# Low halves of one token group's weights: from GpSimd's subtract to VectorE's

## The chip, the cores and the metric

The kernel runs on one core of one Trainium2 chip. A core has five instruction queues: TensorE (PE, matrix products into PSUM), VectorE (DVE), ScalarE (ACT), GpSimd (POOL) and SyncE (SP, which here only issues DMAs). Each queue executes its own instructions in order and they meet through semaphores. The metric is the device time of one execution in microseconds (us); lower is better.

## The reference, cut to what matters

A two-layer decoder step for 1024 prompt tokens and 64 sample tokens, model width 1024, everything in float32. Layer 0 is a gated short convolution beside a 4-head attention over 256 memory rows; layer 1 is latent attention with a paged cache (8192 past positions for each of 8 sequences) beside the same kind of memory attention.

```python
def conv_layer(x, hist, mem_k, mem_v, mem_q_g, norm_g, w_in, conv_w, w_out):
    proj = rms_norm(x, norm_g) @ w_in
    u, gb, gc, q_mem, z = jnp.split(proj, CONV_SPLITS, axis=-1)
    full = jnp.concatenate([hist.astype(x.dtype), gc * u], axis=1)
    conv = sum(conv_w[j] * full[:, j:j + t] for j in range(CONV_WIDTH))
    y_conv = gb * conv
    q = rms_norm(q_mem.reshape(b, t, MEM_HEADS, MEM_HEAD_DIM), mem_q_g)
    y_mem = mem_attend(q, mem_k, mem_v)
    out = jnp.concatenate([y_conv, y_mem], axis=-1) * jax.nn.silu(z)
    return x + out @ w_out, full[:, t:]
...
def mla_layer(x, pos, attend, mem_k, mem_v, ...):
    proj = rms_norm(x, norm_g) @ w_in        # then q, latent kv, memory q and gate z
    o_lat = attend(q_abs, q_pe, ckv, kpe, kscale)
    ...
    return x + out @ w_out, ckv, kpe, kscale
```

## The kernel before

Each large product is made of three matmuls on rounded operands. A float32 operand `a` is split into a high half `h` (ACT rounds `a` to the fp32r type, line 183 in `split`) and a low half `l = a - h` (`sub`, line 179, one subtract with two SBUF inputs). `mm3` (lines 189 to 191) then adds `wh*xh`, `wh*xl` and `wl*xh` in PSUM, so line 191 is the one matmul of the three that needs the weight's low half, line 190 the one that needs the activations' low half.

The prompt is cut in two token groups. Group A holds 256 prompt tokens and the 64 sample tokens (320 columns in a matmul), group B the other 768 prompt tokens (two chunks of 384). Both groups stream the same weights from HBM, each on its own: layer 0's input weights in 40 units of 128x1024 (tiles `wri` raw, `whi` high, `wli` low), layer 0's output weights in 16 units of 128x768 (`wro`, `who`, `wlo`), layer 1's input weights in 19 units of 128x1024 (`wri` again). `Stream.get(i)` (line 318) splits unit i+1 and loads unit i+2 while unit i is used. There are two buffers of each tile: ACT may overwrite `whi` only when PE has finished the unit that lay there, and SP may reload `wri` only when both halves of the unit that lay there have been made.

Which engine makes the halves is set by small tables: the first entry of `A_ENG` (group A), `W_ENG` (group B), `M_ENG` (memory weights, `wlm`) and `O_ENG` (the last output weights) names the engine of the low halves, `"v"` VectorE or `"g"` GpSimd; the second, `"a"`, says that ACT makes the high ones. Group A's low halves are made on GpSimd and group B's on VectorE. In the layer 0 norm, `norm_T2` (line 263) makes the low halves of the eight activation tiles `xL`, every second one by `le`, which is GpSimd. `split_y` (line 712) makes the low halves of twelve output tiles, block 6 (`YG`) on GpSimd.

The program is written as generators that run in two strands: the left one holds the memory keys and values (`mem_kv`), then group B, then the prompt's latent attention; the right one holds group A, then the samples' paged attention. `interleave` (line 1791) alternates the strands by nominal costs in the `yield`s, and when the program is built the framework's scheduler lays the recorded instructions of all strands into one fixed order for each engine, by its own cost model. A change of an instruction's engine therefore moves its neighbours too. On VectorE the order around the change holds, besides the subtracts, chains of very short instructions on [128, 2] tiles (the inverse square roots, lines 202 to 206, tiles `rsq`, `mrs`, `strxb`, `ksr`), the convolution (lines 659 to 682, tiles `vb`, `cv`, `yr`), the softmax steps (lines 493 to 500) and the square sums of group B's norm (line 259, `sqaxb`). GpSimd, besides the subtracts, makes short copies of the convolution's history (lines 648 to 668) and issues the gathers of the paged cache (line 1078).

Of the kernel before, what the change touches and what calls it, by code (L numbers as in the profile page):

```python
# [49 lines left out]
NATB = 4  # L50
RECB = 2
M_ENG = ("vvgv", "a")
A_ENG = ("g", "a")
SCL = "vaaaaaaa"
PSP = "ggg"
W_ENG = ("v", "a")
# [5 lines left out]
VI = (2, 3, 4, 5)  # L62
SLAG = 1
O_ENG = ("g", "a")
YG = (6,)
YORD = [(0, 2)] + [(b, x) for b in (11, 0, 1, 2, 3, 4, 5, 6, 7) for x in range(2)]
YLB = 6
O1I = (0, 1, 2, 4, 6)
# [17 lines left out]
VG0, VG1, VGM, VGQL, VGQ, VGK, VMQ, VCW = 0, 8, 16, 32, 35, 36, 37, 39  # L86
# [6 lines left out]
def build(nc, tc, I, O):  # L93
# [30 lines left out]
    NB = {"v": V, "g": G}[NBE]  # L124
# [26 lines left out]
    def vcol(i):  # L151
        return vec[:, i:i + 1]
# [28 lines left out]
    def split(h, l, src, he="a", le="v"):  # L181
        if he == "a":
            A.activation(h, src, AF.Copy)  # L183
        else:
            V.tensor_copy(h, src)
        sub(V if le == "v" else G, l, src, h)
# [57 lines left out]
        for k in range(8):  # L244
            split_g(xH[:, k, :], xL[:, k, :], xk(k), gcol + k)

    def norm_T(pt, x, gcol, tiles, Tn, xH, xL, tag, le="g", ae=None, load=None):

        acc = pt.tile([128, Tn], F, name="sqa" + tag, tag="sqa")
        A.activation(acc, x[:, 0, :], AF.Square)  # L250
        for k in range(1, 8):
            if load:
                load(k + XAH)
            sq = pt.tile([128, Tn], F, name="sq" + tag, tag="sq", bufs=2)
            if ae and SQB[k % 2] == "g":
                G.tensor_tensor(out=sq, in0=x[:, k, :], in1=x[:, k, :], op=ALU.mult)
            else:
                A.activation(sq, x[:, k, :], AF.Square)
            (ae or V).tensor_tensor(out=acc, in0=acc, in1=sq, op=ALU.add)
            yield 0.0015 * Tn  # L260
        yield from norm_T2(pt, lambda k: x[:, k, :], acc, gcol, tiles, Tn, xH, xL, tag, le)

    def norm_T2(pt, xk, acc, gcol, tiles, Tn, xH, xL, tag, le="g"):
        r = stat_r(pt, [acc], tiles, D, tag)[1]
        yield NY
        rb = bcast_tok(pt, r, tiles, Tn, tag)
        yield 3.0
        for k in range(8):
            xn = pt.tile([128, Tn], F, name="xn" + tag, tag="xn", bufs=2)
            x = xk(k)  # L270
            for c0, n, ps in rb:
                V.scalar_tensor_tensor(out=xn[:, c0:c0 + n], in0=x[:, c0:c0 + n], scalar=vcol(gcol + k), in1=ps[:, 0:n], op0=ALU.mult, op1=ALU.mult)
            split(xH[:, k, :], xL[:, k, :], xn, "a", le if k % 2 else "v")
            yield 0.002 * Tn

    class Stream:
# [351 lines left out]
    def in0(g, xH, xL, ytile, done, pq, last=None):  # L628
# [3 lines left out]
        order = list(range(40)) if g.sample else order  # L632
        ws = Stream(pw, pw, [I["wi0"][u] for u in order], 1024, "i0", *(A_ENG if g.sample else W_ENG))
        pp = P.new("p1c" + str(g.p0))
# [86 lines left out]
    def out0(g, get, xsrc, acc, keep, px=None, held=None, wpre=()):  # L721
# [7 lines left out]
        def weights():  # L729
            p = P.new("p2w" + str(g.p0))  # L730
            ws = Stream(p, p, [I["wo0"][u][:, 768 * j:768 * (j + 1)] for u in range(8) for j in ((1, 0) if px and u == 7 else (0, 1))], 768, "o0", *(A_ENG if g.sample else W_ENG), bufs=2)
            ws.raw.update(enumerate(wpre))
# [946 lines left out]
    def group_b(g, xin):  # L1679
# [3 lines left out]
        xH = px.tile([128, 8, g.T], R, name="xH")  # L1683
        xL = px.tile([128, 8, g.T], R, name="xL")
        pt = L.new("ptb")
        x = pt.tile([128, 8, g.T], F, name="x")
# [5 lines left out]
        for k in range(XAH + 1):  # L1692
            load(k)
            yield 0.5
        yield from norm_T(pt, x, VG0, g.tiles, g.T, xH, xL, "xb", "g", NB, load)
        L.close(1)
        py = L.new("pyb")

# [53 lines left out]
    def layer1(g, N, xH, xL, pq, start=None):  # L1752
# [3 lines left out]
        pw = N.new("pnw" + tag)  # L1756
        ws = Stream(pw, pw, [I["wi1"][u] for u in range(19)], 1024, "i1", *(A_ENG if g.sample else W_ENG))
        if start:
# [193 lines left out]
```

## Time and profile before

| | us |
|---|---|
| median of 3 runs (lowest to highest) | 2034.68 (2033.48 to 2039.29) |
| the profiled execution's own time | 2020.94 |
| span of its instructions | 2019.1 |
| PE busy / VectorE / ScalarE / GpSimd | 1919.3 / 990.9 / 744.9 / 665.0 |

The profiled execution is one execution on the chip, recorded instruction by instruction. Its time is 13.7 us below the median of the runs, so sums over the trace are made against its own time. "Span" runs from the first to the last instruction. PE is busy in 95% of it. [...]

### The profile page before, as it was taken

Reading aid. Unit: us, or ns where it says so; the run is one execution under the profiler, and the core shown is the slowest. Engines: PE = TensorE matmul, PEld = TensorE weight load, DVE = VectorE, ACT = ScalarE, POOL = GpSimd, SP = SyncE. Lnnn points to the kernel's source line nnn. Section 1 sums busy time; section 2 is a strip of 40 time slices with the busy share of each in tenths; the row PEclk is TensorE's granted clock in tenths of the full one; section 3 lists DMA queues with packets and bytes.
Section 4 is the critical chain, followed back from the end, with each engine's and each line's share of the span. In section 5 each row is a group of like instructions: output and inputs, shape, how many; then the busy total and the mean of one; then the engine's idle time right before and its main releaser. Section 6 shows DMA issues by size and latency. Waiting matters only on the chain. (4 is left out here: it accounts for less than half of the span.)

```text
span 2019.1 us, 35721 instructions
## 1 busy us (share of the span) xinstructions
PE 1919.3 (95%) x12508; PEld 1655.5 (82%) x12508; DVE 990.9 (49%) x2578; ACT 744.9 (37%) x1499; POOL 665.0 (33%) x588
## 2 busy tenths in 40 slices
PE   6987999998999999999999999999998899998999
PEld 6987998988997877777788776777787687787999
DVE  7559454456653534444323444445456556657300
ACT  6434323333321133333222422333343666667300
POOL 4544432422220213333333334332322333432220
PEclk8999999989999999999999999999999999999999
DMA  6553535552446378787998888887852211113532
GB/s 223 169 193 91 176 98 211 146 158 87 154 142 217 101 242 284 226 293 250 313 322 286 268 278 293 265 258 247 283 169 69 84 57 58 65 43 129 183 95 73
DMA packets 192884, 368.28 MB, mean 182 GB/s; under 512 B 27809, under 2 KB 135585, under 8 KB 191426
## 3 DMA queue, kind: packets, MB, share of 16 engines
q1 hardware_dynamic: 172178, 298.75, 45.2%
q0 software_dynamic: 20528, 67.26, 10.4%
q8 instruction: 99, 1.62, 0.3%
q14 instruction: 79, 0.65, 0.1%
HBM read 331.22 MB, written 34.70 MB: 181 GB/s over the span
## 5 line engine op out<-in xcount | busy, mean ns | idle before, releaser
L1078 POOL DMA_INDIRECT nat<-nat,IX x256 | 271.6, 1061 | 490.1 <-PE pv L1163 422.6
L189 PE MATMUL mm<-xH,whi 128*128 128x384 f32 (+1 forms) x1112 | 372.7, 335 | 10.6 <-ACT whi L183 5.9
L191 PE MATMUL mm<-xH,wli 128*128 128x384 f32 (+1 forms) x1112 | 367.2, 331 | 6.6 <-POOL wli L179 4.1
L190 PE MATMUL mm<-xL,whi 128*128 128x384 f32 (+1 forms) x1112 | 367.1, 330 | 0.3 <-DVE xL L179 0.3
L189 PEld LDWEIGHTS mm<-xH,whi 128*128 128x128 f32 x1112 | 214.2, 193 | 27.4 <-issue 10.3
L183 ACT ACTIVATE whi<-wri 128x1024 fp32r<-128x1024 f32 (+1 forms) x130 | 126.3, 978 | 265.9 <-PE mm L190 202.3
L191 PEld LDWEIGHTS mm<-xH,wli 128*128 128x128 f32 x1112 | 213.7, 192 | 8.6 <-POOL wli L179 4.9
L190 PEld LDWEIGHTS mm<-xL,whi 128*128 128x128 f32 x1112 | 213.7, 192 | 3.9 <-issue 2.8
L179 POOL TENSOR_TENSOR wli<-wri,whi 128x1024 fp32r<-128x1024 f32 (+1 forms) x65 | 146.7, 2261 | 163.3 <-ACT whi L183 158.1
L1092 PE MATMUL sAB<-rec,qar 128*64 128x256 f32 x1024 | 149.5, 389 | 0.0
L1163 PE MATMUL pv<-nat,PT 128*64 128x256 f32 x1024 | 139.5, 394 | 7.8 <-ACT PT L1143 6.3
L1163 PEld LDWEIGHTS pv<-nat,PT 128*64 128x64 f32 x1024 | 76.3, 139 | 51.0 <-ACT PT L1143 14.3
L1092 PEld LDWEIGHTS sAB<-rec,qar 128*64 128x64 f32 x1024 | 79.5, 138 | 42.6 <-issue 11.5
L179 DVE TENSOR_TENSOR wli<-wri,whi 128x1024 fp32r<-128x1024 f32 (+1 forms) x65 | 73.7, 1136 | 80.3 <-ACT whi L183 79.4
L1107 DVE CUSTOM_DVE_ANT_1 ss<-sAB,rec,mx 128x256 f32<-128x256 f32 x120 | 57.9, 483 | 101.6 <-PE sAB L1097 90.4
L189 PE MATMUL mm<-nH,whi 128*128 128x384 f32 x304 | 104.8, 345 | 0.6 <-ACT whi L183 0.6
L190 PE MATMUL mm<-nL,whi 128*128 128x384 f32 x304 | 102.7, 338 | 0.8 <-DVE nL L240 0.8
L191 PE MATMUL mm<-nH,wli 128*128 128x384 f32 x304 | 102.2, 336 | 0.0
L179 POOL TENSOR_TENSOR wlo<-wro,who 128x768 fp32r<-128x768 f32 (+3 forms) x30 | 59.0, 1975 | 120.4 <-ACT who L183 120.4
L189 PE MATMUL mm<-yHo,who 128*128 128x384 f32 (+1 forms) x288 | 96.9, 337 | 0.9 <-ACT yHo L183 0.9
L191 PE MATMUL mm<-yHo,wlo 128*128 128x384 f32 (+1 forms) x288 | 94.5, 328 | 0.4 <-DVE wlo L179 0.4
L190 PE MATMUL mm<-yLo,who 128*128 128x384 f32 (+1 forms) x288 | 94.0, 326 | 0.4 <-DVE yLo L179 0.4
(594 smaller groups left out, 4335.9 us busy)
## 6 DMA issues: line engine op xcount, KB each, us to landing
rec<-rec SPq DMA_DIRECT2D x512, 192.0 KB
wri<-wi SPq DMA_DIRECT2D x114, 512.0 KB
wro<-wo SPq DMA_DIRECT2D x29, 384.0 KB
smkv<-ckm SPq DMA_DIRECT2D x16, 512.0 KB
smkv<-cvm SPq DMA_DIRECT2D x16, 512.0 KB
wrm<-memw SPq DMA_DIRECT2D x7, 1024.0 KB
wro<-wo SPq DMA_DIRECT2D x7, 768.0 KB
yld<-d_ys SPq DMA_DIRECT2D x8, 544.0 KB
```

The lines of the kernel that those rows point to most:

```text
L179: eng.tensor_tensor(out=out, in0=a, in1=h.bitcast(F), op=ALU.subtract)
L183: A.activation(h, src, AF.Copy)
L189: T.matmul(out, wh, xh, start=first, stop=False)
L190: T.matmul(out, wh, xl, start=False, stop=False)
L191: T.matmul(out, wl, xh, start=False, stop=last)
L1078: G.indirect_dma_start(out=t[:, j % 2, :], out_offset=None, in_=I["nat"], in_offset=bass.IndirectOffsetOnAxis(ap=IX[:, q:q + 1], axis=0), ...
L1092: T.matmul(s[x][64 * ab:64 * ab + 64, 0:256], QA[:, cb, b, :], part(t, cb * 128 + ab * 64)[:, 4 * x:4 * x + 4, :], start=(cb == 0), stop=F ...
L1107: V.tensor_tensor_reduce(out=ss[:, 256 * x:256 * x + 256].rearrange("p (g k) -> p g k", g=4), in0=s[x][:, 0:256].rearrange("p (g k) -> p g ...
L1163: T.matmul(d["v"][64 * ab:64 * ab + 64, 0:256], PT[:, j, ab, :], n[j][:, ab * 256:ab * 256 + 256], start=(i == 0 and j == 0), stop=(i == C ...
```

## The change

`A_ENG` names VectorE instead of GpSimd, so that the 65 subtracts of `wli` and the 19 of `wlo` for group A run on VectorE; the first unit of each of the three streams comes in four quarters. The default of `le` in `norm_T` and `norm_T2` becomes VectorE and the parity test goes, which moves four `xL` subtracts of 128x320 (group A) and four of 128x768 (group B). `YG` becomes empty, which moves block 6's low half in group A's and group B's layer 0 output and in the last output. GpSimd keeps one `wlm` unit in four, the last output's `wlo` and the short chains.

```diff
@@ -50,7 +50,7 @@
 M_ENG = ("vvgv", "a")
-A_ENG = ("g", "a")
+A_ENG = ("v", "a")
 SCL = "vaaaaaaa"
@@ -62,7 +62,7 @@
 O_ENG = ("g", "a")
-YG = (6,)
+YG = ()
@@ -244,7 +244,7 @@
-    def norm_T(pt, x, gcol, tiles, Tn, xH, xL, tag, le="g", ae=None, load=None):
+    def norm_T(pt, x, gcol, tiles, Tn, xH, xL, tag, le="v", ae=None, load=None):
@@ -260,7 +260,7 @@
-    def norm_T2(pt, xk, acc, gcol, tiles, Tn, xH, xL, tag, le="g"):
+    def norm_T2(pt, xk, acc, gcol, tiles, Tn, xH, xL, tag, le="v"):
@@ -270,7 +270,7 @@
-            split(xH[:, k, :], xL[:, k, :], xn, "a", le if k % 2 else "v")
+            split(xH[:, k, :], xL[:, k, :], xn, "a", le)
@@ -1692,7 +1692,7 @@
-        yield from norm_T(pt, x, VG0, g.tiles, g.T, xH, xL, "xb", "g", NB, load)
+        yield from norm_T(pt, x, VG0, g.tiles, g.T, xH, xL, "xb", "v", NB, load)
```

The order on VectorE at the end of group A's first four convolution blocks, where group B's norm begins (`sqaxb` are its square sums, `s_1501` and `yr_435` belong to the convolution, the numbers on `wli` and `whi` tell units apart):

```order
-L259 TENSOR_TENSOR sqaxb<-sqaxb,sqxb 128x768 x3
+L179 TENSOR_TENSOR wli_1503<-wri_1453,whi_1502 128x1024
+L259 TENSOR_TENSOR sqaxb<-sqaxb,sqxb 128x768
 L609 SCALAR_TENSOR_TENSOR s_1501<-slt,mm 128x320
 L259 TENSOR_TENSOR sqaxb<-sqaxb,sqxb 128x768
 L678 SCALAR_TENSOR_TENSOR cv<-s_1501,cv 128x320
+L259 TENSOR_TENSOR sqaxb<-sqaxb,sqxb 128x768 x2
+L682 TENSOR_TENSOR yr_435<-cv,mm 128x320
 L259 TENSOR_TENSOR sqaxb<-sqaxb,sqxb 128x768
-L682 TENSOR_TENSOR yr_435<-cv,mm 128x320
+L179 TENSOR_TENSOR wli_1546<-wri_1506,whi_1545 128x1024
 L259 TENSOR_TENSOR sqaxb<-sqaxb,sqxb 128x768 x2
+L179 TENSOR_TENSOR wli_1599<-wri_1549,whi_1598 128x1024
```

Three weight subtracts now stand between the square sums, which wait for ACT's squares, and the convolution's last steps; before they stood alone on GpSimd.

The order on VectorE in layer 1, where group A's memory head begins (`msq` is the square sum that TensorE waits for, `wli_5034` is a unit of group B, the two `cv` of 128x768 are group B's convolution):

```order
 L671 TENSOR_SCALAR cv<-vb,vec 128x768
+L498 RECIPROCAL mls<-mls 128x2
+L672 SCALAR_TENSOR_TENSOR cv<-vb,vec,cv 128x768
+L500 TENSOR_SCALAR mP<-mP,mls 128x256 x2
+L673 SCALAR_TENSOR_TENSOR cv<-vb,vec,cv 128x768
 L179 TENSOR_TENSOR wli_5034<-wri_4808,whi_5033 128x1024
-L672 SCALAR_TENSOR_TENSOR cv<-vb,vec,cv 128x768
-L673 SCALAR_TENSOR_TENSOR cv<-vb,vec,cv 128x768
 L452 SCALAR_TENSOR_TENSOR msq<-acc_98,msq 128x320
 L179 TENSOR_TENSOR mqL<-mm,mqH 128x256
 L459 COPY mSQ<-msq 128x4x8 x2
+L179 TENSOR_TENSOR wli_4989<-wri_4954,whi_4988 128x1024
```

The same instructions stand ahead of `msq` as before; group A's own subtract, `wli_4989`, now follows it here, and on other heads (`wli_5192`, `wli_5366`) it stands ahead.

## Rows read from the trace of the kernel before

**Rows 1.** Engines over the span, the page: busy us, share, instructions.
```profile
PE 1919.3 (95%) x12508; PEld 1655.5 (82%) x12508; DVE 990.9 (49%) x2578; ACT 744.9 (37%) x1499; POOL 665.0 (33%) x588
```
**Rows 2.** Busy time by stretch (us), then granted clock, DMA share, GB/s.
```profile
0.00:600.00 600.00, 547.93 (x3495) 526.41 (x3496) 354.42 (x742) 222.70 (x418) 222.12 (x166) 0.95 0.47 153
250.00:300.00 50.00, 50.00 (x341) 49.06 (x340) 23.79 (x41) 11.82 (x15) 17.30 (x13) 1.00 0.29 90
```
**Rows 3.** Costliest groups, the page: busy us, mean ns of one, idle before.
```profile
L179 POOL TENSOR_TENSOR wli<-wri,whi 128x1024 fp32r<-128x1024 f32 (+1 forms) x65 | 146.7, 2261 | 163.3 <-ACT whi L183 158.1
L179 DVE TENSOR_TENSOR wli<-wri,whi 128x1024 fp32r<-128x1024 f32 (+1 forms) x65 | 73.7, 1136 | 80.3 <-ACT whi L183 79.4
```
**Rows 4.** Instruction groups by shape, same columns.
```profile
L179 POOL TENSOR_TENSOR wli<-wri,whi 128x1024 fp32r<-128x1024 f32 x57 | 139.6, 2450 | 159.5 <-ACT whi L183 157.6 <-DMA wri<-wi 1.7
L179 DVE TENSOR_TENSOR wli<-wri,whi 128x1024 fp32r<-128x1024 f32 x57 | 69.8, 1225 | 78.5 <-ACT whi L183 77.7 <-DMA rec<-rec 0.7
L179 DVE TENSOR_TENSOR wlo<-wro,who 128x768 fp32r<-128x768 f32 x14 | 13.5, 967 | 35.9 <-ACT who L183 35.8
L179 DVE TENSOR_TENSOR yLo<-yr,yHo 128x320 fp32r<-128x320 f32 x11 | 4.5, 485 | 0.0
```
**Rows 5.** Timeline of DVE and POOL: start, us, instruction.
```profile
53.97 0.17 DVE L205 SCALAR_TENSOR_TENSOR rsq<-rsq,ksv 128x8 f32<-128x8 f32 x1
54.17 2.33 DVE L206 SCALAR_TENSOR_TENSOR ksr<-rsq,ksr 128x8 f32<-128x8 f32 x1
54.07 2.41 POOL L179 TENSOR_TENSOR wli<-wri,whi 128x1024 fp32r<-128x1024 f32 x1 [2.60 <-ACT whi L183]
```
**Rows 6.** Timeline of DVE, first and last of the long ones before 600 us.
```profile
26.49 1.31 DVE L202 TENSOR_SCALAR strxa<-stvxa 128x3 int32<-128x3 int32 x1
...
578.67 2.03 DVE L609 SCALAR_TENSOR_TENSOR z<-slt,z 128x320 f32<-128x320 f32 x1 [0.60 <-ACT slt L608]
```
**Rows 7.** Busy time in four stretches, columns of Rows 2.
```profile
130.00:150.00 20.00, 14.66 (x85) 13.88 (x83) 15.09 (x18) 11.08 (x16) 9.71 (x7) 0.83 0.66 247
150.00:206.00 56.00, 43.45 (x281) 41.17 (x281) 50.93 (x128) 25.63 (x51) 26.15 (x12) 0.94 0.31 92
428.00:445.00 17.00, 15.41 (x79) 14.71 (x78) 12.01 (x51) 3.67 (x10) 3.02 (x2) 0.80 0.34 115
486.00:502.00 16.00, 11.94 (x56) 11.44 (x56) 12.71 (x27) 4.87 (x11) 6.02 (x4) 0.79 0.31 98
```
**Rows 8.** Timeline of PE, instructions before which it stood idle.
```profile
59.34 0.45 PE L189 MATMUL mm<-whm,memH 128*128 128x256 f32 x1 [1.28 <-DVE vb L661]
135.40 0.42 PE L191 MATMUL mm<-xH,wli 128*128 128x320 f32 x1 [1.69 <-POOL wli L179]
140.17 0.41 PE L189 MATMUL mm<-xH,whi 128*128 128x320 f32 x1 [1.27 <-ACT whi L183]
143.10 0.63 PE L191 MATMUL mm<-xH,wli 128*128 128x320 f32 x1 [2.38 <-POOL wli L179]
432.91 0.81 PE L214 MATMUL statcq<-ones,cqacc 128*128 128x2 f32 x6 [1.59 <-DVE cqacc L833]
493.62 0.56 PE L471 MATMUL mst<-ones,msq 128*128 128x2 f32 x2 [3.65 <-DVE msq L452]
```
**Rows 9.** Timeline of DVE and POOL ahead of two of those stalls.
```profile
430.21 2.12 DVE L828 TENSOR_TENSOR cqacc<-cqacc,cqsq 128x320 f32<-128x320 f32 x1
429.41 2.57 POOL L179 TENSOR_TENSOR wli<-wri,whi 128x1024 fp32r<-128x1024 f32 x1 [3.59 <-ACT whi L183]
488.89 3.13 DVE L672 SCALAR_TENSOR_TENSOR cv<-vb,vec,cv 128x768 f32<-128x768 f32 x1
575.61 1.01 DVE L672 SCALAR_TENSOR_TENSOR cv<-vb,vec,cv 128x768 f32<-128x768 f32 x1
```
**Rows 10.** Timeline of ACT, and waits of PE (us in total, times, longest).
```profile
126.33 1.06 ACT L183 ACTIVATE whi<-wri 128x1024 fp32r<-128x1024 f32 x1 [2.94 <-PE mm L190]
PE mm L191 <- DVE wli L179: 2.5, 2, 1.7
```

## The prediction

> **What bounds the kernel now.** The engines' shares come first: TensorE (PE) is busy for 1919.3 of 2019.1 us, VectorE (DVE) for half and GpSimd (POOL) for a third [rows 1]. So the end is set by PE, and an edit on the other engines is worth only the idle time or low clock that it takes from PE. The table by stretch then says where that is. Group A's work with the moved subtracts lies in the first 600 us; there PE is busy for 547.93 us, idle for 52, at a granted clock of 0.95 [rows 2]. In much of it nothing can be won: from 250 to 300 us PE is full at clock 1.00 while GpSimd works 17.30 us of the 50 [rows 2]. After 600 us only two moved instructions are left. What counts is therefore the list of PE's stalls before 600 us, read with what DVE and POOL did just ahead of them.
>
> The groups of instructions give the price of the subtract: 2450 ns for a 128x1024 unit on POOL, 1225 ns on DVE [rows 4]. The timelines of DVE and POOL laid side by side give a second price. On DVE a step on a [128, 8] tile takes 0.17 us; the next one, of the same size, takes 2.33 us, from 54.17 to 56.50, and POOL's `wli` runs from 54.07 to 56.48 [rows 5]. The short step sat through the whole of POOL's subtract. I compared each DVE instruction before 600 us with the short ones of its own shape: 61 take over half a microsecond longer, the first at 26.49 and the last at 578.67 [rows 6], each with a POOL instruction beside it, 102 us in all. Four of these microseconds belong to POOL instructions that stay (memory weights, a fill); 98 us go with the moved ones.
>
> [...]
>
> **The change part by part.** *What DVE gets.* 65 `wli` at 1136 ns mean are 73.7 us (group B's same list of 65 costs that, quarters included [rows 3]); 19 `wlo`, of which 15 at 967 ns and four quarters at about 0.3, 15.7 us; four `xL` and one `yLo` of 320 columns at 485 ns, 2.4 us; four `xL` and one `yLo` of 768 columns, as long as `wlo`, 4.8 us; one last output tile, about 1.3 us [rows 4]. Together 98 us. *What DVE loses*: 98 us of standing blocked. Its load stays as it is. What changes is where it is late: never for 2.4 us behind POOL any more, but for 1.2 us at places that the new order fixes. *What POOL loses*: 65 subtracts of 146.7 us [rows 3] and 30 others. Nothing waits for POOL longer than before, since the short copies that stay follow each other sooner. *Loads*: SP may refill a raw buffer when both halves are made, which comes 2450 - 1225 ns earlier where DVE is free.
>
> Now PE's stalls, stretch by stretch.
>
> 130 to 150 us: group A runs nearly alone, PE is busy 14.66 of 20 us and the clock is 0.83 [rows 7]. Two stalls wait for POOL's `wli`, 1.69 and 2.38 us, and one of 1.27 us for ACT's `whi` [rows 8], which stands behind squares whose sums DVE makes late. A subtract 1.2 us shorter takes 1.2 off each of the two; half of the third goes with DVE's blocking: 3.0 us. [...] Together 4.7. The new order puts `wli_1546` behind the last but two of the square sums, so the bound on the other side is that it gets no faster: 0 to 8.
>
> 150 to 206 us, group A's memory heads beside group B's norm: DVE is busy 50.93 of 56 us and PE idle 12.55 us [rows 7]. DVE is the bound here. Of its 50.93 us, 17.4 are blocked time of the kind above (11 instructions). It gets eight `wli` at 1.225 us and four `xL` at 0.97: 13.7 us. The difference, 3.7 us, comes off the stretch. If the chain of short steps is what limits it, and the subtracts fall beside it, up to 10 is won; if they fall into it at bad places, 3 is lost.
>
> 428 to 445 us: one stall of 1.59 us for `cqacc` [rows 8]. The addition before it took 2.12 us beside POOL's `wli` of 2.57 us [rows 9]; unblocked, an instruction of 320 columns takes 0.485 [rows 4]. The stall goes: 1.6 us. [...] Together 3.3, between 0 and 5.
>
> 486 to 502 us: PE waits 3.65 us for `msq` [rows 8], which stands behind group B's `cv` of 768 columns on DVE. That `cv` took 3.13 us, and 1.01 where nothing blocks it [rows 9]: 2.1 us. What is late next is the rest of the same queue, the two `cv` and `wli_5034`, which stand ahead of `msq` as before; so 1.5 us of the stall remain. Clock 0.79 [rows 7], half of 3.4: 1.7. Together 3.8, between 1 and 7.
>
> The rest: 1.28 us at 59.34 behind two blocked chains [rows 8], and about as much again in group A's later memory heads, where the square sum is blocked in the same way: 2.5 us, 0 to 4. The last output's moved tile (DVE then makes nine in a row instead of eight) lies beside matmuls that use the tiles one by one: nothing.
>
> The gains add up to 4.7 + 3.7 + 3.3 + 3.8 + 2.5 = 18.0 us.
>
> *What is new and late.* A subtract at the head of DVE's queue waits for ACT's `whi`, which waits for PE to free the buffer: ACT stood 2.94 us so before one unit [rows 10]. What stands behind it (the convolution's last steps, the short chains, group B's softmax) waits with it, where POOL's queue kept such a wait to itself. The nearest price is group B, which has run this arrangement all along: its 65 subtracts cost PE 2.5 us in two waits [rows 10]. For 95 moved instructions that is 3.6 us. It is a low estimate, since group B's unit lasts over twice as long on PE; the upper bound is in the slow rival. I take 3.6.
>
> Sum: 2020.94 - 18.0 + 3.6 = 2006.5 for an execution like the profiled one. The median of the runs lies 13.7 us above it, which I carry over: 2020.3, rounded to 2020.
>
> **The rivals.**
>
> *More comes back (2007 us).* Group A's stalls are what makes the clock fall, and all of the falls in the three clocked stretches go: another 5.1 us. The memory heads shorten by 10 instead of 3.7: 6.3 more. The new waits cost 1.6 instead of 3.6: 2 more. For it: each fall of the clock comes right behind a stall on the list. Against it: PE stays idle for some time in each of the stretches. 2020 less 13.4 is 2007.
>
> *DVE swaps one delay for another (2034 us).* 98 us of blocked time against 98 us of subtracts: if PE's critical chains meet a subtract as often as they met a blocking, only the two waits for POOL's `wli` shrink, by 2.4 us, and the 3.6 us of new waits eat that. For it: the load is equal, and DVE is full from 150 to 206 us. Against it: a blocking costs 2.2 us of a short chain and a subtract 1.2.
>
> *Group A's feed gets too tight (2042 us, slower).* A unit of 24 matmuls of 320 columns lasts 3.5 us on PE (341 in 50 us [rows 2]). In that time ACT needs 1.06 us for `whi` [rows 10] and DVE 1.225 for `wli`; 1.2 us are left. Where other DVE work of over 1.2 us stands ahead of the subtract (two square sums of 768 columns, a `cv` of that size and one more step), PE stalls by the excess. If that is as much as 1.2 us in 15 of group A's 75 units, the gain of 18.0 is spent; in 20 of them it is 24 us, and with a clock that stays low as long as before the result is 24 - 18 = 6 us or more above 2034.68. For it: the new order has places where two or three such pieces stand ahead. Against it: in most of the time groups A and B alternate on PE, so that a unit has 7 us or more, and the order was made with the subtracts in it.
>
> [...]
>
> **How the numbers follow.** Forecast (2012 to 2029): 0.46; more comes back: 0.20; swap: 0.20; too tight: 0.14. About 0.3%, 6 us, is what a measurement of this kernel can tell from no change. The first two cases are faster by more than that: 0.66; the third is the same: 0.20; the last slower: 0.14. The range for 8 in 10 leaves out the outer parts of the first and the last rival: 2005 to 2041.
>
> **What would show it right or wrong.** Before 600 us DVE has no short step over 1 us except beside the four `wlm` of POOL, and its busy time stays within 10 us of 354 [rows 2]. PE's waits for POOL's `wli` are gone, those for DVE's `wli` stay under 8 us in all. The stalls at `cqacc` and `msq` fall to under 0.5 and to about 1.5 us. PE's idle time before 600 us falls from 52 to about 40 us and the mean clock there rises to 0.96. Wrong would be: DVE's `wli` in PE's list with 15 us or more, or as many stretches at the low clock as before and an idle time of 50 us.

## The result, and the profile after

The changed kernel takes 2010.07 us (median; 2008.97 to 2021.16) against 2034.68 us: a ratio of 0.9887, 95% interval 0.9861 to 0.9912. It is 24.6 us faster, where 14.7 were forecast.

The execution that was profiled is, at 2021.16 us, the slowest of the five, and that of before was 14 us under its median. So the two spans are equal (2019.4 and 2019.1 us), and the gain isn't seen in them. It is seen in the start of one PE instruction. The first latent-key product, L952, runs just after the last weight of group A. Two timelines of PE, first of before, then of after (start, us, instruction, idle time ahead of it):

```profile
636.21 2.33 PE L952 MATMUL mm<-swk,ckvsT 128*64 128x512 f32 x5 [0.80 <-DMA swk<-wuk]
```
```profile
613.10 2.33 PE L952 MATMUL mm<-swk,ckvsT 128*64 128x512 f32 x5 [0.71 <-DMA swk<-wuk]
```

It starts 23.1 us earlier: all of the gain lies ahead of it. What follows took 2019.1 - 636.2 = 1382.9 us in the one and 1406.3 in the other. None of A's weights is split there, and in the runs below the same remainder lies anywhere between 1378 and 1410 us. It goes mostly with the set of runs: 1378 to 1384 us in the first set below and 1392 to 1410 in the later ones, and the kernel before itself has a median of 2016 us in the first and of 2035 to 2040 in the later ones. PE's list shows a part of what differs here: in the paged attention it waits 6.3 us for `PT` in the profile of before and 13.8 in that of after. Below I therefore compare starts up to L952, and whole times only as ratios.

The page of after and its stretches answer [rows 1, 2, 7] (columns as there):

```profile
PE 1918.3 (95%) x12508; PEld 1653.9 (82%) x12508; DVE 983.4 (49%) x2673; ACT 744.7 (37%) x1499; POOL 474.6 (24%) x493
```
```profile
0.00:600.00 600.00, 560.80 (x3655) 539.83 (x3656) 353.44 (x860) 227.18 (x425) 37.06 (x73) 0.97 0.49 162
130.00:150.00 20.00, 17.18 (x110) 16.65 (x110) 15.96 (x36) 10.76 (x16) 1.32 (x2) 0.91 0.60 206
150.00:206.00 56.00, 46.42 (x292) 44.27 (x291) 48.00 (x138) 29.02 (x57) 1.33 (x6) 0.91 0.43 135
428.00:445.00 17.00, 16.55 (x102) 15.06 (x101) 8.52 (x37) 4.35 (x13) 0.64 (x2) 1.00 0.29 93
486.00:502.00 16.00, 16.00 (x107) 15.96 (x106) 11.50 (x29) 6.39 (x13) 0.00 (x0) 1.00 0.38 116
```

GpSimd's work before 600 us falls from 222 to 37 us, VectorE's stays (354 and 353). PE's idle time there goes from 52 to 39 us, the clock from 0.95 to 0.97. The granted clock of PE is a share, 1.00 the highest; in windows of 1 us before 600 us it reads 1.00 or 0.50 in both traces, and values between the two only where it changes. In the trace of before it is at 0.50 for 6.8 us in each of the three stretches whose mean in [rows 7] is 0.83, 0.80 and 0.79. In that of after, matmuls of 320 columns follow each other every 0.27 us where it reads 0.50 (139.01 to 140.87) and every 0.15 us where it reads 1.00 (144.99 to 146.75). Up to L952, where both kernels have done the same products, VectorE is busy for 367 us before and 359 after, and PE is idle for 52.9 and 39.9. The stretch at 428 us is nearly full and that at 486 us is full, both at clock 1.00; these windows are cut by time, so they hold somewhat later instructions than before. The moved subtracts, against [rows 3, 4], from the page (busy us, mean ns, idle before):

```profile
L179 DVE TENSOR_TENSOR wli<-wri,whi 128x1024 fp32r<-128x1024 f32 (+1 forms) x130 | 147.0, 1136 | 123.9 <-ACT whi L183 122.6
```

The blocking of [rows 5] is gone. The view of the tile `ksr` gives min/median/max in ns of the step that took 2.33 us there:

```profile
L206 DVE SCALAR_TENSOR_TENSOR ksr<-rsq,ksr x6: 156/166/167, 50.1 to 99.7; 128x8 f32<-128x8 f32 x6
```

By the count of [rows 6], 3 instructions before 600 us are over half a microsecond too long instead of 61, 4.6 us in all. Where PE still waits before 600 us, without the two largest, which were there before as well (ACT's `whm` 7.7 us, ACT's `whi` 6.5 us after and 5.9 before); us in total, times, longest:

```profile
PE bcxa L234 <- DVE dgxa L233: 5.9, 1, 5.9
PE mtr L512 <- DVE mP L500: 4.6, 2, 3.1
PE my L189 <- ACT mPTH L183: 3.6, 4, 1.2
PE mm L189 <- ACT wnh L183: 1.8, 1, 1.8
PE mm L191 <- DVE wli L179: 1.8, 3, 1.1
```

Of the six stalls of [rows 8], five are no longer there: those for `vb`, for POOL's `wli` (two), for `cqacc` and for `msq`. The sixth, for ACT's `whi`, was 1.27 us and is now:

```profile
135.54 0.41 PE L189 MATMUL mm<-xH,whi 128*128 128x320 f32 x1 [1.74 <-ACT whi L183]
```

New in the list is the second line, and it shows one chain that now holds PE up between 142 and 284 us. DVE, ACT and PE ahead of the longest of these waits, three timelines:

```profile
189.67 0.15 DVE L206 SCALAR_TENSOR_TENSOR mrs<-rsq,mrs 128x2 f32<-128x2 f32 x1
189.91 1.22 DVE L179 TENSOR_TENSOR wli<-wri,whi 128x1024 fp32r<-128x1024 f32 x1
191.06 0.17 DVE L479 TENSOR_SCALAR mrs<-mrs 128x2 f32<-128x2 f32 x1
191.13 0.95 DVE L179 TENSOR_TENSOR xL<-xnxb,xH 128x768 fp32r<-128x768 f32 x1
192.00 0.16 DVE L494 SCALAR_TENSOR_TENSOR mnb<-mmx,mrs 128x2 f32<-128x2 f32 x1
```
```profile
192.34 1.06 ACT L183 ACTIVATE whi<-wri 128x1024 fp32r<-128x1024 f32 x1 [1.40 <-PE mm L190]
193.31 0.55 ACT L497 ACTIVATE mP<-msc,mnb,mrs 128x256 f32<-128x256 f32 x1
```
```profile
195.48 0.80 PE L512 MATMUL mtr<-ident,mP 128*128 128x128 f32 x4 [3.08 <-DVE mP L500]
```

Three steps of 0.16 us that make `mnb` take 2.5 us, since a subtract of A's weight and one of the norm stand between them in the queue. Then ACT's exponential stands behind a `whi`. PE pays 3.1 us. Nothing is blocked here; the chain waits its turn.

### The profile page after: what moved, and what is told of

It reads as the page before. It is cut to its first block, busy times and chain, and to the rows that moved or that the text cites. A ratio compares the mean times of both kernels' runs of the same rounds, so it can differ in the third digit from the quotient of the medians.

```text
span 2019.4 us, 35704 instructions
## 1 busy us (share of the span) xinstructions
PE 1918.3 (95%) x12508; PEld 1653.9 (82%) x12508; DVE 983.4 (49%) x2673; ACT 744.7 (37%) x1499; POOL 474.6 (24%) x493
## 5 line engine op out<-in xcount | busy, mean ns | idle before, releaser
L189 PEld LDWEIGHTS mm<-xH,whi 128*128 128x128 f32 x1112 | 211.6, 190 | 22.5 <-issue 10.0
L179 DVE TENSOR_TENSOR wli<-wri,whi 128x1024 fp32r<-128x1024 f32 (+1 forms) x130 | 147.0, 1136 | 123.9 <-ACT whi L183 122.6
L1163 PE MATMUL pv<-nat,PT 128*64 128x256 f32 x1024 | 141.0, 397 | 16.6 <-ACT PT L1143 13.8
L183 ACT ACTIVATE who<-wro 128x768 fp32r<-128x768 f32 (+3 forms) x44 | 38.1, 873 | 146.7 <-PE mm L190 115.5
L1434 ACT ACTIVATE ass<-ass,anb,arq 128x128 f32<-128x128 f32 (+3 forms) x64 | 55.4, 866 | 63.6 <-DVE anb L1432 63.6
```

What stands on the lines that cost most here:

```text
L179: eng.tensor_tensor(out=out, in0=a, in1=h.bitcast(F), op=ALU.subtract)
L189: T.matmul(out, wh, xh, start=first, stop=False)
L1163: T.matmul(d["v"][64 * ab:64 * ab + 64, 0:256], PT[:, j, ab, :], n[j][:, ab * 256:ab * 256 + 256], start=(i == 0 and j == 0), stop=(i == C ...
L1434: A.activation(ss[:, 0:kv], ss[:, 0:kv], AF.Exp, bias=nb, scale=d["rq"][:, i:i + 1], accum_out=ls)
```

## The experiments

Twelve runs were made, in four sets; two of them are the kernels before and after once more. The kernel before ran in each set too (medians 2016, 2040, 2035 and 2037 us), and the ratios are to it. Four PE instructions cut the way to L952 into stages: the first `bcxa` (layer 0's norm of group A), the first `statxb` (that of group B), the first `sms` (the sample tokens' memory attention), the first `statcq` (the compressed queries' norm), and L952. Stage II has the memory heads beside group B's norm, stage IV the later heads. Lengths in us, from the starts in each trace. "Blocked" is the time that DVE instructions before 600 us took over the short ones of their shape beside a moved or added GpSimd instruction, where that is over 0.5 us each. Two traces of one kernel differ by up to 2.5 us in a stage (stage IV takes 193.2 us in the profile of after and 190.7 in e2_after), so a difference of that size in one stage says little. Lines that an experiment adds shift the line numbers behind them by 5 or 6 (L479 is L485 in e3_idle).

| kernel | I: bcxa to statxb | II: to sms | III: to statcq | IV: to L952 | L952 starts | blocked | ratio to before, interval |
|---|---|---|---|---|---|---|---|
| e1_before | 115.2 | 149.0 | 135.6 | 203.3 | 635.5 | 57, 97 us | one execution |
| e2_after | 109.0 | 144.0 | 136.2 | 190.7 | 611.0 | 0 | 0.9886 [0.9869, 0.9904] |
| e4_A | 108.6 | 141.9 | 137.6 | 191.7 | 612.1 | 7, 6 us | 0.9879 [0.9861, 0.9896] |
| e5_rest | 113.7 | 149.7 | 134.5 | 200.0 | 629.7 | 55, 94 us | 0.9983 [0.9967, 0.9999] |
| e3_idle | 113.6 | 158.1 | 136.0 | 203.7 | 643.9 | 60, 90 us | 1.0062 [1.0046, 1.0077] |
| e9_copy | 111.1 | 148.2 | 138.6 | 194.2 | 625.3 | 42, 34 us | 0.9936 [0.9914, 0.9958] |
| e12_half | 109.2 | 144.6 | 136.8 | 199.1 | 622.2 | 23, 39 us | 0.9940 [0.9918, 0.9963] |
| e6_twice | 113.0 | 154.0 | 140.3 | 189.8 | 631.7 | 0 | 0.9979 [0.9958, 1.0000] |
| e10_none | 103.4 | 134.1 | 133.0 | 192.8 | 596.1 | 0 | 0.9787 [0.9764, 0.9809] |

**The two kernels again.** 

> The kernel before once more, for a second trace. In the two traces at hand TensorE reaches the first product of the sample group's preparation (line 952, behind the whole of group A) at 636.2 us before and 613.1 us after, 23 us earlier, and yet both executions end within 0.3 us of each other: the profiled execution of before was 14 us faster than its median, the one of after 11 us slower than its median. Theory (the stretch behind 640 us varies from execution to execution, the stretch ahead does not): line 952 starts at 636 +-2 us again, and the rest of the span differs from the first trace's 1383 us by up to 20 us. Rival (the change costs 22 us in the paged attention): the rest is 1383 +-4 us here.

e1_before took 2016.83 us, a single execution. L952 starts at 635.5 us and the rest takes 1379.5 us, which both theories allow. e2_after, unchanged too: 

> The changed kernel once more. Both theories: 20 to 28 us faster than before, ratio 0.987 to 0.991. Theory of a varying rest: line 952 starts at 613 +-2 us, and the rest of the span lies well under the first trace's 1406 us, near 1390. Rival (the change itself costs 22 us behind 640 us): the rest is 1406 +-4 us again.

The ratio came back, 0.9886. L952 starts at 611.0 us and the rest takes 1384.3 us: the rest varies, as the theory said, and the change does not cost 22 us there. The two traces of this set have the gain between them up to L952 (24.5 us), and also one place where some is given back. PE in the paged attention, before and after:

```profile
1281.76 0.44 PE L1163 MATMUL pv<-nat,PT 128*64 128x256 f32 x2 [1.06 <-ACT PT L1143]
```
```profile
1260.95 0.69 PE L1163 MATMUL pv<-nat,PT 128*64 128x256 f32 x2 [5.03 <-ACT PT L1143]
```

How many such waits there are differs between executions of one kernel: ahead of 1570 us 4 with 6.3 us in before and 6 with 8.7 in e1_before, 9 with 13.8 us in after and 4 with 11.2 in e2_after; why stays open.

**Which part of the change?** e4_A takes A's weights alone, e5_rest all but them.

```diff
 before.py -> e4_A                  after.py -> e5_rest
-A_ENG = ("g", "a")                -A_ENG = ("v", "a")
+A_ENG = ("v", "a")                +A_ENG = ("g", "a")
```

e4_A: 

> The kernel before with the low halves of group A's weights alone on VectorE; the norm's and block 6's stay on GpSimd. These are 84 of the 95 instructions and 177 of some 190 us of GpSimd. Theory: line 952 starts at 613 to 619 us and 80 to 100% of the gain is there, 18 to 24 us. Rival (the norms count, since group B's norm lies in the stretch where VectorE is full): line 952 starts at 622 us or later and under 14 us of the gain are there.

e5_rest: 

> The kernel after with group A's low halves given back to GpSimd (A_ENG "g"), so that only the two other parts are changed: every low half of the layer 0 norms and group b = 6 of YG on VectorE. The theory that the whole gain is A's weights: the DVE steps longer than 0.5 us by being blocked stay within 10 of the 57 before 600 us (97 us), and the time is that of the kernel before, ratio 0.998 to 1.002. The rival, that the norm's low halves carry a part (two xL low halves of GpSimd lie beside the chain at 177 to 198 us of before, and 2.1 us there): ratio 0.994 to 0.998. A second rival, that they cost (the norm's chain waits for DVE's subtracts): ratio above 1.002.

A's weights alone give the whole of it, within the intervals. The norms' and `YG`'s low halves alone give 0.2%, just clear of no change (L952 comes 5.8 us earlier than in e1_before), and nothing measurable on top of A's.

**The lock or the slow feed?** e3_idle keeps VectorE's fast subtracts and gives GpSimd an idle one of the same size beside each.

```diff
+                if self.idle:        # the streams i0, i1, o0 of group A
+                    hh = h[:, c:c + q].bitcast(F)
+                    G.tensor_tensor(out=olT[...][:, 0:q], in0=hh, in1=hh, op=ALU.subtract)
```

> As the changed kernel, and GpSimd makes a subtract of the same shape for each of group A's 84 weight pieces again, as soon as the high half is there, into a tile that nothing reads at that time: nobody waits for it. Theory (what was won is VectorE's time of standing blocked beside GpSimd's subtracts): over 70 us of long VectorE steps come back on top of the subtracts that stay on VectorE, line 952 starts at 640 us or later, and the time is that of before or up to 25 us above it. Rival (what was won is the shorter way of the low half, 1.2 us instead of 2.4): the way is still short, line 952 starts at 613 to 618 us and the time is within 5 us of the changed kernel's.

By "lock" I mean what [rows 5] show: a VectorE and a GpSimd instruction that do not run beside each other, so that the second stands until the first ends (there for 2.33 us, in a step that takes 0.17). e3_idle is slower than the kernel before, by 0.6%: PE waits 5.9 us for `wli`, against 1.8 in e2_after, so the feed is still good, but L952 comes 32.9 us later, since VectorE now has the subtracts and the blocking. Up to L952 PE, VectorE and ScalarE execute the same instructions in the same order as in e2_after (3731, 872 and 430 of them), so GpSimd's added instructions are the only difference. They do not slow every engine: ScalarE's `whi` of 128x1024 takes 1058 ns in the kernel before, 1059 after and 1058 here. So the lock is the main thing that the change removes. POOL and DVE in e3_idle, two timelines:

```profile
190.18 2.87 POOL L316 TENSOR_TENSOR olT<-whi 128x1024 f32<-128x1024 f32 x1 [10.94 <-ACT whi L183]
```
```profile
190.07 1.23 DVE L179 TENSOR_TENSOR wli<-wri,whi 128x1024 fp32r<-128x1024 f32 x1 [0.70 <-ACT whi L183]
191.22 1.86 DVE L485 TENSOR_SCALAR mrs<-mrs 128x2 f32<-128x2 f32 x1
```

**Must it have two inputs?** e9_copy has `G.tensor_copy(olT[...][:, 0:q], hh)` in that place; the order on the other engines is again that of e2_after. 

> The kernel after, with a one-input operation of GpSimd beside each piece of group A's weights: a copy of the high half into a buffer that nobody reads then (the run e3_idle had a two-input subtract there). The theory that any GpSimd instruction of this length on such a tile holds VectorE off: some 50 DVE steps are blocked again by about the copy's length and the ratio to the kernel before is 0.998 to 1.008, as for e3_idle. The rival, that only an operation with two inputs does: no DVE step is longer than in the kernel after, ratio 0.987 to 0.992, whatever the copies take on GpSimd.

Neither: the ratio lies between. The same place in its trace, POOL and DVE:

```profile
181.53 2.03 POOL L316 COPY olT<-whi 128x1024 f32<-128x1024 f32 x1 [8.88 <-ACT whi L183]
```
```profile
181.43 1.23 DVE L179 TENSOR_TENSOR wli<-wri,whi 128x1024 fp32r<-128x1024 f32 x1 [1.20 <-ACT whi L183]
182.58 1.00 DVE L485 TENSOR_SCALAR mrs<-mrs 128x2 f32<-128x2 f32 x1
```

A copy blocked as well, but for its own length. Alone the copy of this shape takes 1.04 us, and e3_idle's subtract, which reads one tile twice, 1.89. (The moved subtract reads two tiles and was never under 2.34 us in the kernel before.) Here DVE's subtract is under way, so GpSimd waits first (until 182.66) and then holds VectorE, whose short step ends with it: 181.53 + 2.03 = 183.56 and 182.58 + 1.00 = 183.58. So the lock went to whoever came first, to GpSimd in [rows 5] and to VectorE here, and GpSimd's span of 2.03 us contains its own wait of some 1 us. The mechanism of the first theory holds; its size fell, because I had taken the copy to be as long as the subtract.

**Does VectorE's own load cost?** e6_twice subtracts each of A's low halves twice; e10_none leaves them out and makes only the high halves.

```diff
 e6_twice                                                  e10_none
+                    sub(V, l[...], t[...], h[...])      +   self.hl[self.nsp] = (h, h if self.idle else l)
```

e6_twice: 

> The kernel after, with each low half of group A's weights subtracted twice on VectorE (the second time the same numbers into the same place; PE waits for the second). It adds some 77 us to VectorE before 600 us (84 pieces, 0.92 us each on the average) and nothing to GpSimd. The theory that what counts is the blocking alone, and VectorE has room: its busy time before 600 us rises from 354 to some 430 us, PE's waits for DVE wli rise from 1.8 to 3 to 10 us, and the ratio to the kernel before is 0.989 to 0.996. The rival, that VectorE's own load costs as much as the lock did (a low half and a short chain behind another subtract come late): PE idles 48 us or more before 600 us, ratio 0.999 or more.

The ratio is 0.9979 [0.9958, 1.0000], between the two forecasts and nearer the rival's: my theory that VectorE has room fell. It adds 71 us to VectorE before 600 us (77 up to L952), and L952 comes 20.7 us later. PE idles 49 us before 600 us, as the rival said. Its list there has 6.0 us for `wli`, and these two lines for the short chains behind a pair of subtracts:

```profile
PE mtr L517 <- DVE mv__2155 L482: 4.2, 1, 4.2
PE mtr L517 <- DVE mP L505: 4.2, 3, 2.3
```

e10_none: 

> The kernel after without the low halves of group A's weights: nobody subtracts them, and PE multiplies with the high half in their place (as many products of the same size, other numbers). VectorE loses some 98 us of work before 600 us and GpSimd gains nothing. Theory: from the first statxb product to the 214th product mm<-xL,whi (61 to 63 us in the kernel after, VectorE busy all through it) VectorE sets the length, so its own 15 us of subtracts there cost nearly their length, and elsewhere they are hidden: this stage shrinks by 8 to 13 us, all others before 600 us together by under 4, and the ratio to the kernel before is 0.980 to 0.985. The rival, that a subtract of VectorE's own stands where it would idle and only the lock costs: ratio 0.987 to 0.990, as for the kernel after.

A's weights are 84 of the moved subtracts, 90 us in e2_after; the 98 us of the expectation is the sum of all 95. With them gone, L952 comes 14.9 us earlier than in e2_after, 9.8 of them in stage II; stages I and III give 5.6 and 3.2, stage IV and the start give 3.8 back: 5 in all outside II, a little more than the 4 expected. The shorter stage that the expectation names falls from 63.3 to 53.7 us, 9.6 us for some 15 us of subtracts. In e6_twice and e10_none the builder also laid VectorE's other instructions in another order than in e2_after, so what they cost or give includes that; no run separates the two.

Where the load counts and where only the lock does is seen in the stage tables, side by side (stage II above, stage IV below; columns of [rows 2], each row a kernel: e1_before, e2_after, e6_twice, e3_idle):

```profile
147.69:296.65 148.96, 135.89 (x853) 132.69 (x851) 92.88 (x195) 52.57 (x90) 64.46 (x42) 0.94 0.35 116
...
432.24:635.54 203.30, 195.41 (x1232) 186.16 (x1232) 113.80 (x284) 56.72 (x111) 38.26 (x30) 0.97 0.40 133
```
```profile
140.15:284.13 143.98, 134.41 (x853) 132.17 (x851) 92.47 (x232) 52.67 (x90) 5.27 (x16) 0.95 0.38 122
...
420.30:611.00 190.70, 187.37 (x1227) 178.91 (x1227) 102.52 (x297) 57.36 (x111) 5.07 (x16) 1.00 0.43 142
```
```profile
147.59:301.58 153.99, 138.32 (x853) 135.80 (x851) 115.50 (x254) 53.02 (x90) 7.87 (x16) 0.92 0.36 115
...
441.88:631.73 189.85, 186.14 (x1218) 177.14 (x1216) 114.82 (x310) 57.19 (x111) 10.36 (x16) 1.00 0.43 140
```
```profile
146.07:304.18 158.11, 136.91 (x853) 133.42 (x851) 120.67 (x232) 52.54 (x90) 55.15 (x38) 0.92 0.36 112
...
440.17:643.86 203.69, 194.59 (x1226) 183.76 (x1227) 123.93 (x298) 57.19 (x111) 41.55 (x30) 0.97 0.40 132
```

In stage IV e6_twice has VectorE as busy as the kernel before (114.82 and 113.80 us) and is 13.4 us shorter: there the load is free, and what costs is that GpSimd's lock strikes the step PE is waiting for. In stage II the length rises with VectorE's busy time, which includes the time it stands blocked: 66.8 us of it in e10_none, and 92.5, 115.5 and 120.7 in the last three tables, 134.1, 144.0, 154.0 and 158.1 us long, some 0.4 us for each us. Stage II of e1_before is the exception that shows the lock there too: the same busy time as in e2_after, 5 us longer.

**A dose between.** e12_half gives GpSimd every second piece, `A_ENG = ("gv", "a")`. 

> The kernel after with every second piece of group A's weights subtracted on GpSimd, and the others on VectorE. If each blocked step costs PE alike wherever it stands: half of the 57 blocked steps of before come back (some 28, 48 us) and half of the gain goes, ratio 0.993 to 0.996. If the cost sits in a few places (from statxb to the 214th product mm<-xL,whi, and at msq near 493 us): the ratio goes with what is blocked there, anything from 0.989 to 0.999, and the stages elsewhere keep the length they have in the kernel after within 1 us each.

0.9940, about half. But the stages don't halve: I, II and III are those of e2_after within 0.7 us, and 8.4 of the 11.2 us by which L952 is late are in stage IV. The blocked time did come back in the others: 10 us in stage I, 12 in II, 3 in III and 14 in IV, of 25, 31, 14 and 28 in e1_before. So a blocked step does not cost alike wherever it stands. That is the second theory, the few places, except that of its two places only the stage of `msq` got clearly longer. The order on VectorE is another here too.

**What is left.** e8_psp, `PSP = "vvv"`, `VSP = "vvvv"`: 

> The kernel after, with the prompt's latent attention splitting all its key, query and value tiles on VectorE (PSP "vvv", VSP "vvvv") in place of copy on ScalarE, cast and subtract on GpSimd. If the lock is what counts in this stretch too (from 1570 to 1830 us of the kernel after DVE's short steps L204 to L206 and L1432 stand 0.5 to 1.2 us behind GpSimd's akL, aqL, avL and aqp): GpSimd falls by 25 to 40 us there, the PE stalls for rsq (four of 2.4 to 3.0 us, and some of 0.7 to 0.8) go to under half, and the ratio to the kernel before is 0.980 to 0.986. The rival, that VectorE's chain there gets longer by the splits themselves (two operations of 128x512 from PSUM for each): no change, 0.987 to 0.991, or up to 0.995.

0.9847 [0.9820, 0.9875], 2005.94 us, as expected if the lock counts; the interval overlaps that of e2_after. By PE's starts its attention stretch (from 1568.92 to 1869.47 us in e2_after) is 3.4 us shorter, 297.1 instead of 300.6. It is 301.8 to 305.2 us in the profiles of before and after and in e1_before, which don't have this edit, and 297.6 and 296.8 in the two runs below, which have it. GpSimd falls by 68 us, more than the 25 to 40 expected. PE's five waits for `rsq`, 6.9 us, are gone. Those for the keys' norm have grown from 2.9 us, as in its list from 1550 to 1850 us:

```profile
PE tk L1382 <- DVE aks L206: 9.9, 8, 2.6
```

So a part of the saved waits comes back as waits for VectorE's own queue, as in stage II.

e11_best adds `M_ENG = ("vvvv", "a")`: 

> The kernel after with the last GpSimd low halves beside short chains taken off as well: the memory weights' (M_ENG "vvvv") and the prompt attention's splits as in e8_psp. If the lock at 26 to 30 us is what keeps PE waiting for bcxa (5.9 to 6.0 us in every run so far): that wait falls by 1 to 3 us and the ratio is 0.981 to 0.984. The rival, that this wait hangs on the norm's own chain, or that VectorE's four more subtracts of 1.2 us stand in front of it: the ratio of e8_psp, 0.984 to 0.987, or the wait grows by up to 5 us, 0.987.

0.9846 [0.9821, 0.9871], 2004.21 us: no more in the time than e8_psp, though the wait for `bcxa` does fall by 1.1 us, from 6.0 in e8_psp:

```profile
PE bcxa L234 <- DVE dgxa L233: 4.9, 2, 4.7
```

e13_mP moves one step to ScalarE:

```diff
-                    V.tensor_scalar(out=pt[:, j, :], in0=pt[:, j, :], scalar1=ls[:, j:j + 1], scalar2=None, op0=ALU.mult)
+                    A.activation(pt[:, j, :], pt[:, j, :], AF.Copy, scale=ls[:, j:j + 1])
```

> The kernel of e11_best with one more piece of VectorE's work taken off the stage in which it sets the length: the 16 scalings of the memory probabilities by their sum (mP, L500, 0.35 us each, 8 of them from statxb to the 214th product mm<-xL,whi) go to ScalarE, which is busy half of this stage (31.4 of 63 us), as copies with a scale. If VectorE's work there costs its length: 2.8 us off VectorE, the PE waits for mP (4.7 us, two) fall, this stage shrinks by 2 to 4 us, ratio 0.982 to 0.9845 against 0.9846 of e11_best. The rival, that ScalarE's exponentials and copies stand in the same chain, so that the scaling only changes place (0.35 us on VectorE against some 0.5 us on ScalarE by the rows of L497 and L456): no shorter, ratio 0.984 to 0.987.

2000.39 us, 0.9804 [0.9777, 0.9831], the fastest ratio of a complete kernel. Yet the reason that I gave is not borne out: stage II is 144.4 us against 143.9 in e11_best, L952 starts at 609.6 against 609.2, and PE waits 4.8 us for `mP` as before, now from ACT. Taking load off VectorE doesn't help where the step stays in the same chain. The two ratios come from different sets and their intervals overlap; whether e13_mP is faster than e11_best is open.

## Why the prediction was right, and where it was off

The direction and the mechanism were right: GpSimd's lock on VectorE goes, PE's stalls behind it go, and the new waits are small. The size was 10 us short, in idle time and in clock alike. Up to L952 PE's idle time falls by 13.0 us in the profiles of before and after and by 12.3 in e1_before and e2_after, where the terms without the clock sum to 9.3. The time lost to the lower clock, estimated as one minus the granted clock times the stretch, falls from 27.3 to 18.8 us and from 27.3 to 17.1, where 5.1 was forecast. Together that is 21.5 of 23.1 and 22.5 of 24.5 us. (By the matmuls of 320 columns above, 0.15 against 0.27 us, a microsecond at 0.50 costs 0.45 rather than 0.5, so this estimate is about a tenth high.) The forecast's 5.1 are 1.7 us in each of three stretches, half of the 3.4 us that the same estimate gives for each from [rows 7]. That half would be won was my guess, and no run shows such a share: the clock there is 0.91, 1.00 and 1.00 in the profile of after and in e2_after, which gives 1.6, 3.4 and 3.4 us. The terms, against the same PE instructions in the profiles of before and after, and in e1_before and e2_after:

| term | forecast | profiles of before and after | e1_before and e2_after |
|---|---|---|---|
| to 130 us (part of "the rest") | -1.3 | -3.2 | -3.8 |
| 130 to 150 us | -4.7 | -3.5 | -3.8 |
| 150 to 206 us, measured to the 221 us mark of before | -3.7 | -6.3 | -4.8 |
| 206 to 428 us | 0 | -1.1 | +0.3 |
| 428 to 445 us | -3.3 | +0.1 | -3.3 |
| 445 to 485 us | 0 | -0.2 | -0.5 |
| 486 to 502 us | -3.8 | -7.7 | -7.6 |
| on to L952 (the other part of "the rest") | -1.2 | -1.2 | -1.0 |
| new waits | +3.6 | in the rows above | in the rows above |
| sum | -14.4 | -23.1 | -24.5 |

*486 to 502 us* is the step that was mis-sized. I counted one blocked step ahead of `msq`, the `cv` of 3.13 us [rows 9], and let 1.5 us of the stall stand. The chain that VectorE works through before it has a second one, in the trace of before at

```profile
479.58 2.23 DVE L202 TENSOR_SCALAR mrs<-mv__4885 128x2 int32<-128x2 int32 x1
```

and both go. In the profile of after the same three steps, and then PE's instruction without a wait:

```profile
464.11 0.17 DVE L202 TENSOR_SCALAR mrs<-mv__4885 128x2 int32<-128x2 int32 x1
...
469.73 1.00 DVE L672 SCALAR_TENSOR_TENSOR cv<-vb,vec,cv 128x768 f32<-128x768 f32 x1
...
473.23 0.48 DVE L452 SCALAR_TENSOR_TENSOR msq<-acc,msq 128x320 f32<-128x320 f32 x1
```
```profile
474.68 0.50 PE L471 MATMUL mst<-ones,msq 128*128 128x2 f32 x4
```

From `mv__4885` to `msq` it was 493.00 - 479.58 = 13.4 us, and is 473.23 - 464.11 = 9.1: as much as the 2.1 and the 2.2 us of the two. (One of A's own subtracts, 1.2 us, now stands in this chain as well, and VectorE's wait for ACT's `mP` in it has shrunk from 1.3 to 0.2 us.) The whole stall is gone, and with it the clock's fall: 0.79 [rows 7] to 1.00, 3.4 us where I took half. Reading a stall, I should have added the blocked steps along its whole chain.

*To 130 us*: the stall for `vb` at 59.34 us went, 1.3 us as forecast. In the profile of before a fall of the clock lies there too, which the sum left out: 0.91 from 56 to 76 us, and 1.00 in that of after. In e1_before and e2_after the clock is 1.00 there in both, and 1.4 of the 3.8 us lie ahead of the first `bcxa`.

*130 to 150 us*: the two waits for POOL's `wli` went, but the third, for ACT's `whi`, grew from 1.27 to 1.74 us where half of it was to go, and one of 1.1 us for VectorE's `wli` came. The clock rose to 0.91 (from 0.83), about as forecast.

*428 to 445 us*: 3.3 forecast and 3.3 measured in e1_before and e2_after, and the `cqacc` stall is gone (1.6 us in e1_before). In the profile of after a wait of 1.8 us for `wnh`, in the list above, lies in the way; in e2_after it is 0.8. ACT's `wnh` stood 2.3 us there for the load of `wnr`: the sum has no term for loads that come too late once PE is earlier.

*150 to 206 us*: the sum was 3.7 as blocked time less new subtracts, and 4.8 to 6.3 came. That VectorE's busy time bears on this stretch was right (e6_twice and e10_none), that a subtract costs its whole length was too much: in stage II 25.7 us less work in e10_none gave 9.8 us. The longest stall of the stretch was not on the forecast's list. In the trace of before, DVE, then POOL, then PE:

```profile
178.50 1.75 DVE L204 TENSOR_TENSOR rsq<-mrs 128x2 f32<-128x2 f32 x1
180.29 2.26 DVE L205 SCALAR_TENSOR_TENSOR rsq<-rsq,mv__1978 128x2 f32<-128x2 f32 x1
...
183.34 0.48 DVE L609 SCALAR_TENSOR_TENSOR yr<-slt,mm 128x320 f32<-128x320 f32 x1
```
```profile
178.40 1.84 POOL L179 TENSOR_TENSOR xL<-xnxb,xH 128x768 fp32r<-128x768 f32 x1
180.19 2.34 POOL L179 TENSOR_TENSOR wli<-wri,whi 128x1024 fp32r<-128x1024 f32 x1
```
```profile
183.87 0.63 PE L189 MATMUL mm<-xH,whi 128*128 128x320 f32 x1 [3.62 <-DVE yr L609]
```

`yr` stood behind two blocked steps of 0.16 us, and PE waited 3.6 us for it; after the change it doesn't.

*The new waits*: 1.8 us for `wli` instead of 3.6. The price was taken from group B's two waits [rows 10], and both lay behind the lock itself. DVE, POOL and PE at the second of them, in the trace of before:

```profile
210.62 2.63 DVE L671 TENSOR_SCALAR cv<-vb,vec 128x256 f32<-128x256 f32 x2
```
```profile
210.56 2.37 POOL L179 TENSOR_TENSOR wli<-wri,whi 128x1024 fp32r<-128x1024 f32 x1
```
```profile
213.64 0.69 PE L191 MATMUL mm<-xH,wli 128*128 128x384 f32 x1 [1.69 <-DVE wli L179]
```

After the change the two are down to 0.2 us: these 2.5 us were a gain to be counted, and they were taken as the price. But the `wli` waits are not all that is new. What the moved subtracts cost is in the chains behind them: PE waits 4.6 us for `mP` and 1.3 for `mv__1978` after, where it waited 3.5 us for two `mv` of such chains before. The forecast named those that would wait and priced only PE's direct waits.

*The same load on VectorE*: 98 us against 98 holds roughly (354 and 353 us before 600 us; up to L952 it falls by 8). What fell is the reading of the rival "swap" that the two might then cost the same. (Its own sum is 2.4 gained and 3.6 lost, 2036 us rather than 2034.) Against e2_after, 90 us of blocking cost 32.9 us up to L952 in e3_idle, 0.36 of each us, and 90 us of A's subtracts on VectorE 14.9 us (e10_none), 0.17. The second set of subtracts in e6_twice cost 0.29 of each us. e10_none and e6_twice have another order on VectorE, so whether the price rises with the load is not shown. Without any price the runs say: the move with the lock left in (e3_idle) reaches L952 8.4 us later than e1_before, and taking the lock away from it gives 32.9, which makes the 24.5 us measured. How the 8.4 divide among VectorE's added work, the new order and the shorter feed is open.

*The clock*: it is 1.00 in two of the four stretches and 0.91 from 130 to 150 us; from 150 to 206 us it is 0.91, where it was 0.94 before. The rival "more comes back" had 2007 us and lay nearer than the forecast, for the clock and for `msq`, not for its 10 us at the memory heads. *Too tight a feed* did not come: `wli` waits of 1.8 us.

The tests named: VectorE's short steps over 1 us only beside `wlm`, busy time before 600 us within 1 us, no wait for POOL's `wli`, `cqacc` gone, idle 39 us, clock 0.97 (0.96 forecast): as said. `msq` at 1.5 us: wrong, it is gone. The 13.7 us between the profile and the median were carried over. The stretch behind L952 differs by as much between the sets, so they fit there, where the change moves next to nothing; no trace of an execution of before near its median shows it.

*The lock* showed in the other direction as well: in e9_copy the copy, 1.04 us alone, took 2.03 behind VectorE's subtract, and VectorE's short step ended with the copy (183.58 and 183.56 us).

## What to carry to other kernels

A subtract that is moved to an idle GpSimd was not free here (e3_idle 1.0062 against e2_after 0.9886), and a copy was not either (e9_copy 0.9936): look beside each of its instructions for VectorE steps that are longer than others of their shape, and add them up along the chain to the stall. Then ask of the move back whether VectorE's queue has a gap where the work will stand: where a stage's length rises with VectorE's busy time (stage II here, some 0.4 us for each us), the gain is smaller, and the place in the queue counts. And compare two profiled executions up to a common instruction rather than by their spans.

## What the runs showed that was not expected

- In e3_idle and e9_copy GpSimd waited for VectorE too, and the trace counts this wait as its busy time: a subtract of [128, 1024] spans 2.87 us behind a VectorE subtract and 1.89 us alone, a copy 2.03 and 1.04 us.
- In e9_copy a one-input GpSimd copy held short VectorE steps off as well: 42 steps by 34 us, and 0.5% of the time (0.9936 against 0.9886).
- The stretch behind L952 took 1377.7 us (e4_A) to 1409.6 us (e6_twice) with the same work in it, mostly by the set of runs. That is more than the change is worth.
